# ScalarE copies a projection out of PSUM before VectorE convolves it

## The chip, the cores and the metric

The kernel runs on one core of a Trainium2 chip. The metric is the device time of one execution in microseconds (us); before, the median of three executions is 715.25 us. One execution was also taken by the hardware profiler, and every row shown here is from that one.

Five engines work side by side, each on a queue of its own, in order: TensorE (PE in the rows, its weight loads PEld), VectorE (DVE), ScalarE (ACT), GpSimd (POOL), and SyncE (SP), which issues the DMAs. An engine waits for another at a semaphore. PE writes its results into PSUM; ACT and DVE read them from there, POOL can't.

## The reference, cut to what matters

Two decoder layers over 256 tokens of width 1024. Each projects its input x, and part of that projection (q, k and v of a gated delta rule, four heads of 128 columns each) goes through a causal convolution of width 4 and a SiLU:

```
proj = x @ w_in
qkv  = silu(causal_dwconv(concat(q, k, v), conv_w))      # conv_w: 4 taps per column
beta, g = gates(a_logit, b_logit)
o_a  = gated_delta_rule(l2norm(q), l2norm(k), v, g, beta) # chunks, a triangular solve
o_b  = block-sparse softmax attention (partial rotary, own block)
x    = LN(alpha * x + concat(o_a, o_b) @ w_out)
x    = LN(alpha * x + (silu(gate) * val) @ w_down)        # gate, val: conv of width 3 of x @ w_up
```

## The kernel before, in words

Each layer has a mixing stage (projections, delta rule, attention, output projection) and a feed-forward stage. All 256 tokens are held at once: a projection (`proj`) makes one 128 x 256 result, the 128 columns of one head on the partitions and the tokens along the free dimension, in 24 matmuls. Operands are split into a high and a low part (`xh`, `xl`, `wh`, `wl`), so that three products of a fast format give the precision; ACT makes the high part of each weight chunk (line 196) and DVE or POOL the low part (line 197), two instructions of 512 columns each. Five chunks of `wh` and of `wl` can be ready ahead.

Results of projections lie in the PSUM pool `pj`, which has two buffers. So a projection can start only when the one two before it has been read out for the last time.

`gdn_conv` (lines 421 to 430) convolves one result, and it runs 24 times: 4 heads each of k, v and q in 2 layers. ACT writes `cv`, the result times the last tap (L424). DVE adds the other three taps one after the other, each reading the result in PSUM shifted by one to three tokens (L427, three instructions of 255, 254 and 253 columns). ACT takes a tanh of `cv` (L429), and DVE writes `dst` (L430), a slice of `ka`, `va` or `qa`; `va` is the tile that the rows name vz.

What follows on k: products of k with itself (`u_kk`), their scaled form (`u_am`), which goes through DRAM into the triangular solve of 16 x 16 blocks (`u_solve`): 28 small instructions a layer on POOL (L527, L529) and a copy (L530). Its result goes to DRAM (`dx`, L531) and back (L538), is spread by DVE (`u_ex`, L543), and then PE can put the blocks together (`u_lt`, L560, and what follows). POOL also does the second half of the rotary step (L455, L456) and half of the gate's cumulative products (L418).

The order of work is written out: `ORDER` lists the units of each layer, and `@` with letters says on which engines a unit must come behind the one before it. Where no letter binds, the order of the instructions on an engine is decided when the program is built, by what is expected to be ready first; the rows show DVE working weight splits (L197) in between the convolution steps.

Of the kernel before, what the change touches and what calls it, by code (L numbers as in the profile page):

```python
# [16 lines left out]
AF = mybir.ActivationFunctionType  # L17
OP = mybir.AluOpType
# [5 lines left out]
S = 256  # L24
# [65 lines left out]
def hybrid_kernel(ctx, tc, xT, x, wab, wch, par, lnrow, cst, msk, out):  # L90
    nc = tc.nc
    pe, act, dve, pool, sp = nc.tensor, nc.scalar, nc.vector, nc.gpsimd, nc.sync
# [20 lines left out]
    def ps_p():  # L113
        return ps_w()[:, 0:S]
# [226 lines left out]
    for l in range(DEPTH):  # L341
# [10 lines left out]
        def mt(name, shape, bufs=1, dt=F32):  # L352
            return (early if name in EARLY else mix).tile(shape, dt, name=name, bufs=bufs)
# [67 lines left out]
        def gdn_conv(ps, ct, dst):  # L421
            w = pr[:, P_GCONV + 4 * ct:P_GCONV + 4 * ct + 4]
            cv = mt("cv", [128, S], 2)
            act.activation(cv, ps, AF.Copy, scale=w[:, 3:4])  # L424
            for j in (2, 1, 0):
                o = 3 - j
                dve.scalar_tensor_tensor(cv[:, o:], ps[:, :S - o], w[:, j:j + 1], cv[:, o:], op0=OP.mult, op1=OP.add)  # L427
            th = mt("th", [128, S], 2)
            act.activation(th, cv, AF.Tanh, scale=0.5)  # L429
            dve.scalar_tensor_tensor(dst, th, 1.0, cv, op0=OP.add, op1=OP.mult)  # L430

        def u_conv(c0, ct, dst, h):
            ps = ps_p()
            proj(ps, l, c0 + h)
            gdn_conv(ps, ct + h, dst[:, h, :])
# [449 lines left out]
        for j in range(2, FJ):  # L885
            cs = []
            for gi in range(2):
                ps = ps_p() if j > 2 or gi else head
# [115 lines left out]
```

## Time and profile before

| | |
|---|---|
| median of three executions | 715.25 us (714.67 to 718.54) |
| the profiled execution | 714.04 us |
| its span, first to last instruction | 712.3 us |
| PE, DVE, ACT, POOL busy | 97%, 81%, 56%, 28% of the span |
| mean granted TensorE clock | 0.984 of full speed |

The profiled execution took 1.7 us more than its span, and 1.2 us less than the median. A share of busy time is a mean over stages with different limits, and a busy PE is not always PE at its full speed: matmuls overlap, and at half clock they last longer.

### The profile page before, as it was taken

What the parts mean: (1) busy time and instruction counts of PE and PEld (TensorE: products, weight loads), DVE (VectorE), ACT (ScalarE), POOL (GpSimd) and SP (SyncE); (2) the same over time, 40 slices, a digit from 0 to 9 for tenths busy, and PEclk for the clock granted to TensorE, in tenths of its full rate; (3) what the DMA queues carried; (4) which work ended last, traced back from release to release, by engine and by line L of the source; (5) the groups of instructions that cost most, each with busy time, mean ns of one, the idle gap of its engine ahead of it and who ended that gap; (6) DMA issues with size and microseconds to landing.
All of it is one profiled execution on the core that took longest, in us unless ns stands there. A gap on an engine that the chain in (4) does not pass through costs nothing.

```text
span 712.3 us, 13664 instructions
## 1 busy us (share of the span) xinstructions
PE 688.6 (97%) x5056; PEld 618.6 (87%) x5056; DVE 576.9 (81%) x1273; ACT 400.8 (56%) x908; POOL 197.2 (28%) x200
## 2 busy tenths in 40 slices
PE   8989999999999999999999989999999999999994
PEld 5979888787999999999888988888789999999994
DVE  5899877599788887778879987776998888887756
ACT  5644466546666665656355445556476566666531
POOL 0045700013333343332002382000153333333413
PEclk9999999999999999999999997999999999999998
DMA  8876351521766665656153437134246766666201
GB/s 313 305 244 192 78 198 40 199 89 61 276 220 194 211 222 184 202 181 205 60 201 129 144 94 222 61 103 159 66 150 234 233 213 194 214 206 202 70 1 60
DMA packets 41217, 118.07 MB, mean 166 GB/s; under 512 B 10176, under 2 KB 12992, under 8 KB 40640
## 3 DMA queue, kind: packets, MB, share of 16 engines
q1 hardware_dynamic: 41152, 117.21, 49.6%
q8 instruction: 40, 0.66, 0.3%
q14 instruction: 25, 0.20, 0.1%
HBM read 114.84 MB, written 2.36 MB: 165 GB/s over the span
## 4 chain that ended last, share of the span: by engine, by line
PE 86%; DVE 9%; ACT 1%; issue 1%; DMA 1%; SPq 0%; DVEq 0%; ACTq 0%
PE pj L211 16%; PE pj L212 15%; PE pj L214 15%; PE ac L732 8%; PE ac L733 8%; PE ac L734 8%; DVE wl L197 3%; PE pj L225 1%; PE pj L222 1%; DVE cv L427 1%; PE mx L619 1%; PE pj L223 1%; PE mx L313 1%; DMA wr<-in_wch_dram 1%; PE mx L662 1%
## 5 line engine op out<-in xcount | busy, mean ns | idle before, releaser
L196 ACT ACTIVATE wh<-wr 128x512 fp32r<-128x512 f32 x376 | 219.5, 622 | 108.2 <-PE pj L212 49.1
L211 PE MATMUL pj<-xh,wh 128*128 128x256 f32 x1024 | 258.6, 289 | 7.4 <-DVE cv L427 7.4
L212 PE MATMUL pj<-xl,wh 128*128 128x256 f32 x1024 | 257.2, 287 | 0.0
L197 DVE TENSOR_TENSOR wl<-wr,wh 128x512 fp32r<-128x512 f32 x292 | 206.7, 736 | 28.2 <-ACT wh L196 14.7
L211 PEld LDWEIGHTS pj<-xh,wh 128*128 128x128 f32 x1024 | 198.6, 194 | 11.4 <-issue 5.4
L212 PEld LDWEIGHTS pj<-xl,wh 128*128 128x128 f32 x1024 | 199.1, 194 | 1.6
L197 POOL TENSOR_TENSOR wl<-wr,wh 128x512 fp32r<-128x512 f32 x84 | 116.2, 1405 | 204.9 <-ACT wh L196 199.7
L214 PE MATMUL pj<-xh,wl 128*128 128x256 f32 x1024 | 147.6, 286 | 0.0
L214 PEld LDWEIGHTS pj<-xh,wl 128*128 128x128 f32 x1024 | 134.2, 194 | 0.4 <-issue 0.2
L733 PE MATMUL ac<-wh,fal 128*128 128x512 f32 x144 | 56.4, 392 | 0.0
L732 PE MATMUL ac<-wh,fah 128*128 128x512 f32 x144 | 56.1, 392 | 0.0
L734 PE MATMUL ac<-wl,fah 128*128 128x512 f32 x144 | 56.0, 389 | 0.0
L842 DVE TENSOR_TENSOR fal<-fth,fah 128x256 fp32r<-128x256 f32 (+1 forms) x48 | 36.8, 767 | 17.3 <-ACT fah L841 17.0
L828 DVE SCALAR_TENSOR_TENSOR fc<-pj,par,fc 128x255 f32<-128x255 f32 x80 | 38.1, 476 | 4.2 <-ACT fc L824 2.8
L828 DVE SCALAR_TENSOR_TENSOR fc<-pj,hw,fc 128x255 f32<-128x255 f32 x80 | 38.3, 478 | 3.7 <-ACT fc L824 2.4
L817 POOL TENSOR_SCALAR hw<-par 128x66 f32<-128x66 f32 x2 | 2.1, 1048 | 139.2 <-DVE wlh L197 139.2
L839 DVE SCALAR_TENSOR_TENSOR fth<-fth,fc 128x256 f32<-128x256 f32 (+1 forms) x48 | 23.6, 492 | 20.1 <-ACT fth L838 20.1
L841 ACT ACTIVATE fah<-fth 128x256 fp32r<-128x256 f32 (+1 forms) x48 | 18.9, 393 | 34.8 <-DVE fth L840 34.8
L838 ACT ACTIVATE fth<-fc 128x256 f32<-128x256 f32 (+1 forms) x48 | 19.2, 400 | 31.7 <-DVE fc L828 31.5
L427 DVE SCALAR_TENSOR_TENSOR cv<-pj,par,cv 128x255 f32<-128x255 f32 (+2 forms) x72 | 33.8, 472 | 0.6 <-ACT cv L424 0.3
L734 PEld LDWEIGHTS ac<-wl,fah 128*128 128x128 f32 x144 | 27.1, 188 | 5.9
L732 PEld LDWEIGHTS ac<-wh,fah 128*128 128x128 f32 x144 | 27.1, 189 | 4.8
(257 smaller groups left out, 1030.5 us busy)
## 6 DMA issues: line engine op xcount, KB each, us to landing
wr<-in_wch_dram SPq DMA_DIRECT2D x195, 512.0 KB, 4.1
lnb<-in_lnrow_dram SPq DMA_DIRECT2D x4, 1024.0 KB, 4.6
xres<-in_x_dram SPq DMA_DIRECT2D x2, 512.0 KB, 6.8
da<-A SPq DMA_DIRECT2D x4, 256.0 KB, 3.4
ka<-in_wch_dram SPq DMA_DIRECT2D x2, 512.0 KB, 4.5
qa<-in_wch_dram SPq DMA_DIRECT2D x2, 512.0 KB, 5.1
qb<-in_wch_dram SPq DMA_DIRECT2D x2, 512.0 KB, 4.8
kb<-in_wch_dram SPq DMA_DIRECT2D x2, 512.0 KB, 5.7
```

The costliest lines, as they stand in the source:

```text
L196: ih = act.activation(h[:, s], raw[:, s], AF.Copy)
L197: il = le.tensor_tensor(lo[:, s], raw[:, s], h[:, s].bitcast(F32), op=OP.subtract)
L211: pe.matmul(ps, h[:, k, :], xh[:, k, :], start=k == 0, stop=False)
L212: pe.matmul(ps, h[:, k, :], xl[:, k, :], start=False, stop=False)
L214: pe.matmul(ps, lo[:, k, :], xh[:, k, :], start=False, stop=k == KT - 1)
L427: dve.scalar_tensor_tensor(cv[:, o:], ps[:, :S - o], w[:, j:j + 1], cv[:, o:], op0=OP.mult, op1=OP.add)
L732: pe.matmul(ps, a_h, w_h[:, ns], start=start and i == 0, stop=False, skip_group_check=True)
L733: pe.matmul(ps, a_l, w_h[:, ns], start=False, stop=False, skip_group_check=True)
L734: pe.matmul(ps, a_h, w_l[:, ns], start=False, stop=stop and i == len(items) - 1, skip_group_check=True)
L828: dve.scalar_tensor_tensor(cv[:, d], ps[:, d.start - o:d.stop - o], w[:, q:q + 1], cv[:, d], op0=OP.mult, op1=OP.add)
L839: dve.scalar_tensor_tensor(th, th, 1.0, cg[:, ts], op0=OP.add, op1=OP.mult)
L842: dve.tensor_tensor(al, th, ah.bitcast(F32), op=OP.subtract)
```

## The change

ACT first copies the whole result from PSUM into `dst`, then makes `cv` as before. The three DVE steps read the copy in `dst` (SBUF) in place of PSUM. The last step overwrites `dst` as before. Nothing else is changed, `ORDER` and the convolution of the feed-forward stage (`ffn_conv`, L828) included.

```
         def gdn_conv(ps, ct, dst):
             w = pr[:, P_GCONV + 4 * ct:P_GCONV + 4 * ct + 4]
             cv = mt("cv", [128, S], 2)
+            act.activation(dst, ps, AF.Copy)
             act.activation(cv, ps, AF.Copy, scale=w[:, 3:4])
             for j in (2, 1, 0):
                 o = 3 - j
-                dve.scalar_tensor_tensor(cv[:, o:], ps[:, :S - o], w[:, j:j + 1], cv[:, o:], op0=OP.mult, op1=OP.add)
+                dve.scalar_tensor_tensor(cv[:, o:], dst[:, :S - o], w[:, j:j + 1], cv[:, o:], op0=OP.mult, op1=OP.add)
             th = mt("th", [128, S], 2)
             act.activation(th, cv, AF.Tanh, scale=0.5)
             dve.scalar_tensor_tensor(dst, th, 1.0, cv, op0=OP.add, op1=OP.mult)
```

## Rows read from the trace of the kernel before

**Rows 1.** Windows: us, then busy us per engine, granted clock, DMA share, GB/s.

```profile
20.00:70.00 50.00, 48.13 (x373) 45.67 (x371) 49.25 (x139) 28.13 (x62) 18.87 (x17) 1.00 0.72 241
...
500.00:695.00 195.00, 194.71 (x1318) 179.74 (x1317) 158.97 (x294) 114.85 (x233) 62.36 (x47) 1.00 0.50 162
```

**Rows 2.** Costliest groups: busy us, mean ns, idle before and its releasers.

```profile
L211 PE MATMUL pj<-xh,wh 128*128 128x256 f32 x1024 | 258.6, 289 | 7.4 <-DVE cv L427 7.4
...
L427 DVE SCALAR_TENSOR_TENSOR cv<-pj,par,cv 128x255 f32<-128x255 f32 (+2 forms) x72 | 33.8, 472 | 0.6 <-ACT cv L424 0.3
```

**Rows 3.** Timeline of PE: start, us, instruction, idle before it and its releaser.

```profile
72.05 0.43 PE L211 MATMUL pj<-xh,wh 128*128 128x256 f32 x1 [2.08 <-DVE cv L427]
...
419.14 0.36 PE L211 MATMUL pj<-xh,wh 128*128 128x256 f32 x1 [2.04 <-DVE cv L427]
...
435.45 0.36 PE L211 MATMUL pj<-xh,wh 128*128 128x256 f32 x1 [1.48 <-DVE cv L427]
```

**Rows 4.** Windows behind those three waits, columns as in rows 1.

```profile
72.00:76.00 4.00, 3.95 (x20) 3.98 (x21) 2.79 (x6) 1.05 (x3) 3.29 (x10) 0.57 0.14 53
420.00:424.00 4.00, 4.00 (x23) 3.73 (x22) 2.15 (x5) 1.46 (x3) 3.22 (x11) 0.57 0.03 6
437.00:447.00 10.00, 10.00 (x151) 9.34 (x148) 6.55 (x21) 4.97 (x17) 0.00 (x0) 0.52 0.72 264
```

**Rows 5.** Timeline of ACT, ahead of the first of those waits.

```profile
67.28 0.46 ACT L424 ACTIVATE cv<-pj,par 128x256 f32<-128x256 f32 x1
```

**Rows 6.** Single lines of the kernel: ns min/median/max, first and last start, forms.

```profile
L427 DVE SCALAR_TENSOR_TENSOR cv<-pj,par,cv x72: 463/471/484, 24.3 to 459.4; 128x255 f32<-128x255 f32 x24, 128x254 f32<-128x254 f32 x24, 128x253 f32<-128x253 f32 x24
...
L721 DVE SCALAR_TENSOR_TENSOR PT<-mx,par,zs x4: 737/740/741, 146.9 to 497.9; 128x512 f32<-128x512 f32 x4
...
L271 DVE SCALAR_TENSOR_TENSOR xres<-xres,lnr,lnb x14: 740/748/923, 159.5 to 708.4; 128x512 f32<-128x512 f32 x14
...
L442 DVE SCALAR_TENSOR_TENSOR zs<-th,pj x8: 407/412/420, 111.4 to 495.1; 128x256 f32<-128x256 f32 x8
...
L430 DVE SCALAR_TENSOR_TENSOR vz<-th,cv x8: 408/464/566, 72.4 to 433.5; 128x256 f32<-128x256 f32 x8
...
L450 DVE TENSOR_TENSOR kb<-kb,kt x8: 419/884/1005, 45.2 to 405.9; 128x256 f32<-128x256 f32 x8
...
L447 ACT ACTIVATE qb<-pj x8: 363/366/383, 30.2 to 411.5; 128x256 f32<-128x256 f32 x8
```

**Rows 7.** Windows of line 427 alone: DVE busy us (count), clock, DMA share, GB/s.

```profile
36.09:39.56 3.47, 1.33 (x3) 1.00 0.34 137
66.06:81.72 15.66, 4.68 (x10) 0.89 0.23 71
81.78:86.81 5.03, 2.36 (x5) 1.00 0.48 128
```

**Rows 8.** Timeline of POOL within the solve of the first layer.

```profile
74.13 0.29 POOL L529 TENSOR_TENSOR P<-P,T 64x50 f32<-64x50 f32 x1
...
78.11 0.36 POOL L529 TENSOR_TENSOR P<-P,T 64x50 f32<-64x50 f32 x1
...
78.87 0.61 POOL L529 TENSOR_TENSOR P<-P,T 64x44 f32<-64x44 f32 x1
```

**Rows 9.** Timeline of DVE beside four POOL instructions of the second layer.

```profile
430.20 3.00 DVE L197 TENSOR_TENSOR wl<-wr,wh 128x512 fp32r<-128x512 f32 x1
```

**Rows 10.** Timeline of SP: the solve's result is fetched.

```profile
85.32 0.38 SPq L538 DMA_DIRECT2D PT<-dx  x1
...
432.32 0.38 SPq L538 DMA_DIRECT2D PT<-dx  x1
```

**Rows 11.** That line's DMAs, from issue to landing.

```profile
DMA to landing us min/median/max: 3.2/3.3/3.3
```

**Rows 12.** Timeline of DVE: the result is spread, in each layer.

```profile
90.98 0.42 DVE L543 TENSOR_TENSOR gX<-PT,kt 128x256 f32<-128x256 f32 x1
...
436.19 0.42 DVE L543 TENSOR_TENSOR gX<-PT,kt 128x256 f32<-128x256 f32 x1
```

More of the change, by code (lines that the diff above doesn't have):

```diff
@@ L423, in gdn_conv @@
             cv = mt("cv", [128, S], 2)
+            act.activation(dst, ps, AF.Copy)
             act.activation(cv, ps, AF.Copy, scale=w[:, 3:4])
@@ L426, in gdn_conv @@
                 o = 3 - j
-                dve.scalar_tensor_tensor(cv[:, o:], ps[:, :S - o], w[:, j:j + 1], cv[:, o:], op0=OP.mult, op1=OP.add)
+                dve.scalar_tensor_tensor(cv[:, o:], dst[:, :S - o], w[:, j:j + 1], cv[:, o:], op0=OP.mult, op1=OP.add)
             th = mt("th", [128, S], 2)
```

## The prediction

> **What bounds the kernel now.** I read the windows by stage first. In the feed-forward stage PE is busy for 194.71 of 195 us at full clock, and nothing of the change runs there [rows 1]. All 24 convolutions lie in the mixing stages. In the first 50 us of the first one DVE is busy for 49.25 us and PE for 48.13 [rows 1]: two engines at their limit, DVE a little more so. The reader should keep that in mind, because a PE that is let go earlier there gains only what DVE can follow.
>
> The groups show the wait that the change is about. The first matmul of a projection stood idle for 7.4 us in all, and every bit of it was ended by L427, the convolution's last read of the PSUM buffer [rows 2]. The timeline of PE has the three large ones, 2.08, 2.04 and 1.48 us [rows 3]; smaller ones make up the other 1.8. Behind each of the three the granted clock is not 1.00 but 0.57, 0.57 and 0.52 [rows 4]: PE had been idle, and then runs mostly at 1.2 GHz instead of 2.4.
>
> **What the change removes: the wait for the buffer.** After it the last reader of the PSUM buffer is ACT's `cv`. Ahead of the first large wait, `cv` was made at 67.28 in 0.46 us [rows 5]; with a copy of 0.366 in front [rows 6] the buffer is free at 67.28 + 0.37 + 0.46 = 68.1, and PE, idle from 72.05 - 2.08 = 69.97 [rows 3], finds it free. So I expect all of these waits on DVE to go: 7.4 us. If PE isn't idle it should keep its clock: 4 x 0.43 = 1.7 us behind the first wait, 1.7 behind the second, 10 x 0.48 = 4.8 behind the third [rows 4]. The most that can be won is 7.4 + 3.4 + 4.8 = 15.6 us.
>
> **What holds PE next.** A little later in each layer PE needs the result of the solve, and that runs on POOL and through DRAM, not through the buffers. Its fetch was issued at 85.32 and 432.32 [rows 10], and landed 3.3 and 3.2 us later [rows 11], at 88.6 and 435.5. DVE spread it at 90.98 and 436.19 [rows 12]. So this gate can come forward by 2.4 us in the first layer and 0.7 in the second, 3.1 together, and no more. What else PE wins ahead of the gate is worth something only if later projections fill it. I take the 3.1 and half of the rest of waits and first two clock losses, (7.4 + 3.4 - 3.1) / 2 = 3.9, so 7.0. Of the 4.8 behind the third wait I take nothing: the gate of 436.19 lies just ahead of that stretch, and PE has to wait for it anyway.
>
> **What it adds on ACT.** 24 copies of 0.366 us, the price of L447, the same copy of the same shape [rows 6]: 8.8 us. ACT works for 28.13 of the 50 us [rows 1], so most are covered by its idle time. A copy delays the first DVE step only where DVE stands waiting for `cv`: 0.3 us of idle time in all 72 steps [rows 2], one place. I count one copy, 0.4 us; with all cover gone it would be 8.8. Behind the copy on ACT's queue stand `cv`, the weight splits and the tanh; the copy itself stands behind the tanh of the convolution before it, which waits for DVE, so a late DVE can still hold a buffer through ACT.
>
> **What it does to a DVE step.** A step takes 471 ns, and it reads PSUM, SBUF and a per-partition tap [rows 6]. The same operation on 512 columns with such a per-partition scalar takes 740 ns with one input in PSUM (L721) and at least 740, 748 in the middle, with both in SBUF (L271). Without that scalar it takes 407 at least with an input in PSUM (L442) and 408 with none (L430) [rows 6]. So the 63 ns between 471 and 408 go with the scalar, not with PSUM, and I price the move at 0; if they did go with PSUM, 72 x 0.063 = 4.5 us of DVE would fall away. The Trainium skill says the opposite: VectorE: DVE Perf Modes, "The TRN2 errata", lists 58 cycles of fixed cost from SBUF against 120 from PSUM, by which a step would lose 65 ns, an estimate, and the sum below 4.7 us. The pairs of rows don't bear it out.
>
> **What a step is now exposed to.** Reading PSUM, no step of 72 took longer than 484 ns [rows 6], though many ran beside POOL. DVE instructions with both inputs in SBUF do take longer there: L450, started just where POOL does its rotary step, has 419 at best and 884 in the middle [rows 6], and one weight split beside four POOL instructions in a row took 3.00 us [rows 9]. Here the Trainium skill agrees: SBUF — State Buffer, "Who interferes with whom", has a VectorE instruction with two SBUF inputs shut out while GpSimd reads SBUF, and the other way round. It speaks against this change, and these rows have it too.
>
> Counting the steps beside POOL: in the first layer 3 beside L418, 10 beside the solve, 5 beside its copy and the rotary step [rows 7]. In the second layer the same windows hold 3, 10 and 2. That is 13 beside large POOL instructions and 20 beside small ones. A large one costs 884 - 419 = 465 ns if DVE loses, 0 if POOL yields: 0 to 6.0 us. I take half, 3.0. A small one costs 464 - 408 = 56 ns (L430 on vz, which lies in the solve [rows 6]), up to 1.1 us; I take 0.6, because DVE has slack in part of that stretch.
>
> POOL loses as well. In the solve a POOL instruction takes 0.29 us alone, 0.36 beside L430 and 0.61 beside a weight split [rows 8]. Twenty more instructions like L430 make the solve later by 20 x 0.07 = 1.4 us over both layers; if each cost what a weight split costs, 20 x 0.32 = 6.4. A step has L430's columns, so I take 1.4, all of it on the gate.
>
> **The sum.** 714.04 - 7.0 + 0.4 + 0.0 + 3.0 + 0.6 + 1.4 = 712.4 us for an execution like the profiled one; the median lies 1.2 above it, so 713.6. A measurement of this kernel can tell about 0.5%, 3.6 us, from no change; this is 0.2%, no change. The order on each engine is decided anew at the build from what should be ready, so single instructions will trade places; I have no row for that and let the range carry it.
>
> **The rivals.** *The solve becomes late (slower).* If POOL gets to the port only between DVE's instructions, the solve takes 3.2 us longer in each layer, past the slack of 2.4 and 0.7: 0.8 + 2.5 = 3.3 us. The 6 steps beside L418 and the rotary step behind it lie ahead of the products that feed the solve, 6 x 0.465 = 2.8. PE, earlier or not, waits at the gate: 714.04 + 3.3 + 2.8 + 0.4 = 720.5, median 721.7. For it: L450's 884 and the 3.00. Against: L430 beside the solve lost only 56 ns. It decides once the solve is later by more than the slack, 3.1 us over both layers.
>
> *The buffers were the bound (faster).* PE's 7.4 and 3.4 us are won in full, because projections fill PE up to the gate and DVE spreads the result as soon as it lands: 714.04 - 10.8 + 0.4 + 3.0 + 0.6 = 707.2, median 708.4. For it: PE's waits had no other releaser. Against: DVE's 49.25 of 50 us.
>
> *The steps get shorter (faster).* PSUM, not the scalar, is what costs 63 ns: 4.5 us less on the engine that is at its limit, median 709.1. Against it stand the two pairs in rows 6. It is what the Trainium skill's table of fixed costs in VectorE: DVE Perf Modes would do here.
>
> **How the numbers follow.** Forecast 0.44, late solve 0.26, buffers 0.20, shorter steps 0.10. The forecast's own range is 708.5 to 718.5: bounds of the port's price, 3.0 either way, and the order, some 2 more. Of its 0.44, 0.07 lies below the 0.5% and 0.05 above. Faster: 0.07 + 0.19 + 0.08 = 0.34; slower: 0.05 + 0.23 = 0.28; the rest, 0.38, within. The range takes in the middles of the rivals: 705.5, 2.9 below the buffers' time, since the 4.8 of the third clock loss may come in part, to 722.0.
>
> **What would show it.** Right: no wait of PE on L427's successor, and clock 1.00 behind where the first two waits were; the copy at about 0.366 us x24; steps of 471 ns at best, with some of 0.7 to 1 us beside POOL; L543 between 89 and 92 and near 436. Wrong: steps near 410 ns (shorter steps); a solve that ends over 1.6 us later in a layer and a PE idle ahead of L560 (late solve); L543 well ahead of those times, or PE's saving kept to the end of the mixing stage (buffers); or another order on DVE that delays the products of k.

## The result, and the profile after

| | before | after |
|---|---|---|
| median | 715.12 us (4 executions) | 725.91 us (725.06 to 727.29, 4 executions) |
| ratio after / before | | 1.0148, 95% interval 1.0123 to 1.0173 |
| profiled execution, its span | 714.04, 712.3 us | 726.01, 724.2 us |
| mean granted clock | 0.984 | 0.975 |

The change makes the kernel 10.8 us slower, 3.9 us above the range's upper end. Throughout, ratios leave out executions over 1.5% slower than the fastest of their kernel (only three of g2's ten are), and medians are of all of them. In the changed kernel the lines behind 423 have numbers higher by one: the copy is L424, `cv` L425, a step L428, `dst` L431, the solve L528, L530 and its copy L531, the fetch L539, the spreading L544, and the gate of PE L561.

The waits on the buffers are gone. The group that answers to [rows 2], from the page of the changed kernel:

```profile
L211 PE MATMUL pj<-xh,wh 128*128 128x256 f32 x1024 | 259.0, 289 | 1.8 <-ACT cv L425 1.8
```

None of the 7.4 us that DVE ended is left; ACT ends 1.8. But PE waits longer than before, in another place. Its waits, summed by line, with the number of times and the longest:

```profile
PE ac L561 <- DVE gX L544: 14.9, 2, 8.7
```

and in PE's timeline, idle time and releaser in brackets:

```profile
92.52 0.96 PE L561 MATMUL ac<-gX,A 64*64 64x32 f32 x14 [6.18 <-DVE gX L544]
...
447.07 0.43 PE L561 MATMUL ac<-gX,A 64*64 64x32 f32 x4 [8.75 <-DVE gX L544]
```

Before, PE came to this gate with 0.03 and 0.15 us of idle time. Windows of all engines behind it, columns as in [rows 1]; the granted clock follows the five busy times:

```profile
92.00:96.00 4.00, 3.48 (x38) 3.13 (x38) 3.96 (x11) 1.23 (x4) 0.00 (x0) 0.50 1.00 389
96.00:104.00 8.00, 8.00 (x121) 7.67 (x122) 3.57 (x12) 4.13 (x17) 0.00 (x0) 0.50 0.46 174
104.00:110.00 6.00, 6.00 (x102) 4.61 (x102) 3.32 (x9) 4.14 (x12) 0.00 (x0) 0.98 0.00 0
447.00:456.00 9.00, 8.93 (x146) 8.25 (x147) 6.92 (x22) 4.23 (x16) 0.00 (x0) 0.50 0.88 322
456.00:460.00 4.00, 4.00 (x24) 3.87 (x24) 1.38 (x3) 1.27 (x3) 0.00 (x0) 0.59 0.00 0
```

In layer 1 the clock was 1.00 from 92 to 110 us before; now PE is at 1.2 GHz for 12 us. In layer 2 it ran at half clock before as well [rows 4], now for some 2 us more (12.2 us from the gate on, against 10.2).

The gate is late because the solve is. POOL's timeline: first instructions and closing copy of the solve in both layers, after:

```profile
66.18 1.20 POOL L528 TENSOR_TENSOR T<-T,P 64x14 f32<-64x14 f32 x1 [2.71 <-DVE P L525]
67.46 3.56 POOL L530 TENSOR_TENSOR P<-P,T 64x14 f32<-64x14 f32 x1
...
84.89 0.97 POOL L531 COPY P<-P 64x256 f32<-64x256 f32 x1
...
420.77 0.60 POOL L528 TENSOR_TENSOR T<-T,P 64x14 f32<-64x14 f32 x1 [0.92 <-DVE P L525]
...
439.60 0.84 POOL L531 COPY P<-P 64x256 f32<-64x256 f32 x1
```

and the same of the kernel before, not shown yet:

```profile
66.06 2.14 POOL L527 TENSOR_TENSOR T<-T,P 64x14 f32<-64x14 f32 x1 [1.88 <-DVE P L524]
...
81.78 1.07 POOL L530 COPY P<-P 64x256 f32<-64x256 f32 x1
...
412.82 0.60 POOL L527 TENSOR_TENSOR T<-T,P 64x14 f32<-64x14 f32 x1 [1.07 <-DVE P L524]
...
428.80 1.07 POOL L530 COPY P<-P 64x256 f32<-64x256 f32 x1
```

From the first start to the copy's end: 85.86 - 66.18 = 19.68 and 440.44 - 420.77 = 19.67 us after, 16.79 and 17.05 before: 2.89 and 2.62 longer, 5.5 together. In layer 1 the gate had a slack of 2.4 us (DMA landed at 88.6, spreading at 90.98 [rows 11, 12]); now the spreading follows the DMA at once. DVE's own queue ahead of it ended at 91.89 us, 0.1 us before the DMA landed at 92.0, so in layer 1 both were late. The fetch and the spreading, from SP's and DVE's timelines, answering to [rows 10] and [rows 12]:

```profile
88.32 0.38 SPq L539 DMA_DIRECT2D PT<-dx  x1
...
442.89 0.38 SPq L539 DMA_DIRECT2D PT<-dx  x1
```

```profile
92.04 0.42 DVE L544 TENSOR_TENSOR gX<-PT,kt 128x256 f32<-128x256 f32 x1
...
440.52 2.93 DVE L431 SCALAR_TENSOR_TENSOR qa<-th,cv 128x256 f32<-128x256 f32 x1 [0.54 <-ACT th L430]
446.59 0.42 DVE L544 TENSOR_TENSOR gX<-PT,kt 128x256 f32<-128x256 f32 x1 [3.13 <-DMA PT<-dx]
```

The first operation of layer 1's first norm, on DVE, before and after:

```profile
154.26 0.68 DVE L246 SCALAR_TENSOR_TENSOR xres<-xres,ac 128x512 f32<-128x512 f32 x1
...
160.67 0.68 DVE L246 SCALAR_TENSOR_TENSOR xres<-xres,ac 128x512 f32<-128x512 f32 x1
```

So the 12.0 us between the spans (712.26 and 724.24 us) lie here: first gate 92.04 - 90.98 = 1.1; from it to that norm 5.3 (68.6 against 63.3 us), the way that holds the stretch at half clock; from there to the second gate 4.0, of which the solve is 2.6 and the products of k ahead of it 1.5; behind the second gate 1.6 (277.65 against 276.07). From layer 1's norm to the start of layer 2 it is 212.8 us in both.

The steps themselves, as single lines (ns min/median/max), beside POOL's two lines of the solve after, and the same two before:

```profile
L428 DVE SCALAR_TENSOR_TENSOR cv<-ka,par,cv x24: 468/476/1256, 23.8 to 396.0; 128x255 f32<-128x255 f32 x8, 128x254 f32<-128x254 f32 x8, 128x253 f32<-128x253 f32 x8
L428 DVE SCALAR_TENSOR_TENSOR cv<-vz,par,cv x24: 469/483/522, 70.3 to 436.4; 128x255 f32<-128x255 f32 x8, 128x254 f32<-128x254 f32 x8, 128x253 f32<-128x253 f32 x8
L428 DVE SCALAR_TENSOR_TENSOR cv<-qa,par,cv x24: 471/480/485, 83.2 to 471.5; 128x255 f32<-128x255 f32 x8, 128x254 f32<-128x254 f32 x8, 128x253 f32<-128x253 f32 x8
...
L530 POOL TENSOR_TENSOR P<-P,T x28: 298/461/3562, 67.5 to 439.1; 64x14 f32<-64x14 f32 x4, 64x26 f32<-64x26 f32 x4, 64x36 f32<-64x36 f32 x4, 64x44 f32<-64x44 f32 x4
...
L528 POOL TENSOR_TENSOR T<-T,P x28: 289/418/2781, 66.2 to 438.7; 64x14 f32<-64x14 f32 x4, 64x26 f32<-64x26 f32 x4, 64x36 f32<-64x36 f32 x4, 64x44 f32<-64x44 f32 x4
```

```profile
L529 POOL TENSOR_TENSOR P<-P,T x28: 209/320/1829, 68.3 to 428.5; 64x14 f32<-64x14 f32 x4, 64x26 f32<-64x26 f32 x4, 64x36 f32<-64x36 f32 x4, 64x44 f32<-64x44 f32 x4
...
L527 POOL TENSOR_TENSOR T<-T,P x28: 225/274/2139, 66.1 to 428.2; 64x14 f32<-64x14 f32 x4, 64x26 f32<-64x26 f32 x4, 64x36 f32<-64x36 f32 x4, 64x44 f32<-64x44 f32 x4
```

In the median a step is no shorter than the 471 ns of [rows 6]; DVE pays 5 to 12 ns of a step, and POOL's medians rise from 320 to 461 and from 274 to 418 ns.

### The profile page after: what moved, and what is told of

Its sections match the earlier page's. It is cut to its first block, busy times and chain, and to the rows that moved or that the text cites. A ratio compares the mean times of both kernels' runs of the same rounds, so it can differ in the third digit from the quotient of the medians.

```text
span 724.2 us, 13666 instructions
## 1 busy us (share of the span) xinstructions
PE 689.3 (95%) x5056; PEld 621.0 (86%) x5056; DVE 585.3 (81%) x1273; ACT 407.4 (56%) x932; POOL 203.4 (28%) x200
## 4 chain that ended last, share of the span: by engine, by line
PE 82%; DVE 7%; POOL 5%; DMA 3%; issue 1%; ACT 1%; SPq 0%; DVEq 0%; ACTq 0%
PE pj L211 14%; PE pj L214 14%; PE pj L212 14%; PE ac L733 8%; PE ac L734 8%; PE ac L735 8%; POOL P L530 2%; POOL T L528 2%; DVE wl L197 2%; DVE cv L428 2%; PE pj L225 1%; PE pj L222 1%; PE pj L223 1%; PE mx L313 1%; PE mx L620 1%
## 5 line engine op out<-in xcount | busy, mean ns | idle before, releaser
L839 ACT ACTIVATE fth<-fc 128x256 f32<-128x256 f32 (+1 forms) x48 | 19.2, 400 | 32.6 <-DVE fc L829 32.5
L734 PEld LDWEIGHTS ac<-wh,fal 128*128 128x128 f32 x144 | 27.2, 189 | 4.5 <-DVE fal L843 0.2
```

The source lines that it names most:

```text
L734: pe.matmul(ps, a_l, w_h[:, ns], start=False, stop=False, skip_group_check=True)
L839: act.activation(th, cg[:, ts], AF.Tanh, scale=0.5)
```

## The experiments

Theory A: a step with both inputs in SBUF holds POOL up, the solve ends late, and PE, let go early, stands idle at the gate and loses its clock. Theory B: the order that the build chose is what costs. Theory C: the copies cost by themselves. "Solve" is the time from the end of DVE's mask ahead of the solve to the end of POOL's copy, "idle" PE's idle time ahead of its first matmul behind the gate, each for layer 1 and 2.

| kernel | solve us | idle us | median us | ratio to before, 95% |
|---|---|---|---|---|
| before | 16.9, 17.1 | 0.0, 0.1 | 714.2 to 716.3 | |
| after | 19.8, 19.8 | 6.2, 8.7 | 725.9 | 1.0148 (1.0123 to 1.0173) |
| e1_copy_only | 17.0, 16.4 | 0.0, 0.0 | 715.5 | 1.0032 (0.9998 to 1.0066) |
| e2_v_from_psum | 16.3, 18.1 | 0.0, 3.9 | 726.7 | 1.0170 (1.0143 to 1.0198) |
| e3_v_by_copy | 19.7, 19.3 | 4.7, 7.7 | 723.4 | 1.0125 (1.0105 to 1.0146) |
| f1_change_old_order | 19.7, 19.6 | 4.7, 7.8 | 725.1 | 1.0121 (1.0082 to 1.0160) |
| f2_before_new_order | 15.8, 16.8 | 0.5, 2.2 | 717.4 | 1.0020 (0.9992 to 1.0048) |
| f4_v_psum_old_order | 16.9, 18.1 | 1.4, 4.2 | 720.6 | 1.0069 (1.0042 to 1.0097) |
| e6_cv_in_psum | 17.5, 16.1 | 4.9, 5.5 | 729.1 | 1.0163 (1.0105 to 1.0222) |
| e4_after_fill | 19.8, 19.8 | 4.3, 4.0 | 733.5 | 1.0270 (1.0245 to 1.0295) |
| g1_after_fill | 19.8, 19.8 | 0.1, 0.2 | 719.9 | 1.0083 (1.0052 to 1.0115) |
| g2_cv_psum_fill | 17.5, 16.1 | 0.3, 0.0 | 717.3 | 1.0003 (0.9964 to 1.0041) |
| g3_before_fill | 17.9, 17.9 | 0.1, 1.7 | 715.6 | 1.0016 (0.9991 to 1.0041) |
| i1_after_z_ahead | 19.6, 19.2 | 2.3, 2.4 | 752.3 | 1.0497 (1.0457 to 1.0538) |
| i2_cv_psum_z_ahead | 17.9, 16.6 | 1.9, 3.5 | 742.9 | 1.0378 (1.0328 to 1.0427) |
| i3_cv_psum_one_z | 17.9, 17.1 | 2.8, 3.8 | 733.4 | 1.0257 (1.0196 to 1.0319) |
| j1_before_qa0_behind | 17.0, 16.4 | 0.1, 0.0 | 718.7 | 1.0030 (1.0002 to 1.0059) |
| j2_after_qa0_behind | 19.4, 19.8 | 9.1, 8.5 | 727.5 | 1.0162 (1.0132 to 1.0191) |

### Which part of the change costs

**e1_copy_only** keeps the copies, with the steps reading PSUM:

```
+            act.activation(dst, ps, AF.Copy)
             act.activation(cv, ps, AF.Copy, scale=w[:, 3:4])
...
                 dve.scalar_tensor_tensor(cv[:, o:], ps[:, :S - o], w[:, j:j + 1], cv[:, o:], op0=OP.mult, op1=OP.add)
```

> The ScalarE copies of PSUM into the result's tile stay, but VectorE's steps go on reading PSUM, so that the buffers come free as late as before the change. Theory A (steps with both inputs in SBUF slow GpSimd's solve, and the gate behind it opens late): the solve takes about 17 us in each layer again (19.75 after the change), PE meets the gate as before, and the time is 714 to 717 us. Theory B (the order in which the scheduler lays out the instructions is what changed the time): part of the loss stays, 718 us or more, with a solve of 17 us. Theory C (the copies themselves load ScalarE): most of the 10.8 us of loss stays, 722 us or more.

The solve is back to 17.0 and 16.4 us and the time within 0.7% of before: theory C falls, up to the 0.66% that the interval leaves. Two of its ten executions, 722.4 and 723.4 us at a mean clock of 0.97, lie near the change. Two things are seen besides. Its gates open later than before (PE's first matmul behind them at 92.82 and 441.23 us, against 91.45 and 436.66) at no cost, since PE had work up to them: a late gate alone is no loss where PE has work to do until then. And this kernel also keeps the buffers as late as before, so it doesn't tell the second SBUF input from the early buffers; e6 does.

**e2_v_from_psum** and **e3_v_by_copy** split the 24 convolutions. Those of v, four in each layer (the expectations say eight, which is both layers), lie beside the solve:

```
+            src = ps if 4 * 2 <= ct < 4 * 3 else dst      # e2; in e3 the two names change places
+            if src is dst:
+                act.activation(dst, ps, AF.Copy)
...
-                dve.scalar_tensor_tensor(cv[:, o:], ps[:, :S - o], w[:, j:j + 1], cv[:, o:], op0=OP.mult, op1=OP.add)
+                dve.scalar_tensor_tensor(cv[:, o:], src[:, :S - o], w[:, j:j + 1], cv[:, o:], op0=OP.mult, op1=OP.add)
```

> Only the convolutions of k and q go by the copy; the eight of v in a layer, whose steps lie beside the solve, read PSUM as before the change. Theory A: the solve is back at 17 to 17.5 us in each layer, and 5 us or more of the 10.8 us of loss go, so 714 to 720 us. Theory B or C: the solve can be back, but the time stays within 3 us of the changed kernel's 726.

> The complement: only v's eight convolutions of a layer go by the copy, k and q read PSUM. Theory A: the solve takes 19 to 20 us as after the change, and at least half of the loss is there, 720 to 726 us. Theory B or C: with a third of the copies, a third of the loss or less, 715 to 719 us, whatever the solve takes.

e3 is as A has it: v alone brings the long solve and 8.7 us (723.4 against 714.7 beside it). e2 is not: its solve is short in layer 1, yet it is as slow as the change. There DVE spread the solve's result at 96.57 us, though the DMA had landed at 88.2. DVE was still at q's steps and weight splits, in an order that the build had chosen for this kernel, and one closing step of v had taken 3.63 us beside POOL (82.02 us). So order had to be separated from the operands.

### The order of the instructions

In the next three kernels the order on PE, DVE, ACT and POOL is written out and enforced, instruction by instruction:

```
+def keep_order(nc, tc, nosync):
+    for name, text in QUEUES.items():          # one list of positions for each engine
...
+        for a, b in zip(order, order[1:]):
+            tc.add_manual_dep(ins[b], ins[a].name, nosync, reason="kept order")
```

**f1_change_old_order** is the change in the order of before, **f2_before_new_order** the kernel before in the order of after, and **f4_v_psum_old_order** is e2 in the order of before.

> The change, with the order of all instructions of PE, VectorE, ScalarE and GpSimd fixed to that of the kernel before (the 24 copies stand just ahead of the ScalarE instruction that they preceded). Theory A (the steps' second SBUF input slows GpSimd's solve and with it the gate): the solve takes about 19.7 us in each layer, and the time is 718 to 726 us. Theory B (the order that the build chose is what costs): the solve may be long, but the time is 713 to 717 us.

> The kernel before, without the copies, with the order of all instructions of PE, VectorE, ScalarE and GpSimd fixed to that of the changed kernel. Theory A: the solve takes about 17 us, and the time stays at 713 to 719 us (buffers come free later than the order assumes, some us of waits). Theory B: 722 us or more, with a solve of 17 us and PE idle or waiting ahead of the gate.

> Copies for k and q alone (v's convolutions read PSUM), with the order of the kernel before. In its own order this kernel took 726.7 us although its solve of layer 1 took only 16.3 us. Theory A with the order as a second cause: the solve takes 16 to 17.5 us in both layers and the time is 711 to 716 us. If the copies of k and q cost in another way than by the order, the time stays above 720 us.

f1 loses 1.2% with no instruction out of its old place, and f2 0.2%, which can't be told from nothing. Theory B falls for the change. PE at f1's two gates, and the windows behind them:

```profile
94.57 0.42 PE L673 MATMUL ac<-gX,A 64*64 64x32 f32 x3 [4.65 <-DVE gX L656]
...
447.94 0.42 PE L673 MATMUL ac<-gX,A 64*64 64x32 f32 x4 [7.80 <-DVE gX L656]
```

```profile
94.00:104.00 10.00, 9.43 (x148) 8.76 (x149) 6.05 (x17) 5.67 (x21) 0.00 (x0) 0.50 0.82 302
448.00:456.00 8.00, 8.00 (x142) 7.32 (x143) 5.11 (x14) 4.05 (x15) 0.00 (x0) 0.50 0.95 359
```

f4 stands between, against the 711 to 716 expected: 6 us faster than e2, so e2's order had cost that much, but still 0.7% slower than before. DVE's timeline at the end of the solve in both layers, and POOL's rotary step beside it:

```profile
84.01 3.00 DVE L309 TENSOR_TENSOR wl<-wr,wh 128x512 fp32r<-128x512 f32 x1
...
433.22 3.62 DVE L542 SCALAR_TENSOR_TENSOR cv<-qa,par,cv 128x254 f32<-128x254 f32 x1
```

```profile
85.03 1.43 POOL L571 TENSOR_TENSOR qb<-qb,sw 128x256 f32<-128x256 f32 x2
...
435.14 1.41 POOL L571 TENSOR_TENSOR qb<-qb,sw 128x256 f32<-128x256 f32 x2
```

Here it is DVE that is held. In layer 2 a step of q, 0.47 us elsewhere, took 3.62 and ended 0.3 us after POOL's run of large instructions; the spreading there came with its DMA (440.0 us) all the same. In layer 1 the one held was a weight split, as in layer 2 of the kernel before [rows 9], and the first spreading stands at 93.19 us, though the DMA had landed at 89.5. So the copies of q explain one long step, and what f4's 0.7% consists of stays open.

### The second SBUF input

**e6_cv_in_psum** is the change with the steps' sum in PSUM, so that each step has one input in SBUF:

```
-            cv = mt("cv", [128, S], 2)
+            cv = ps_a()[:, 0:S]
```

> The change, but the tile in which the steps add up lies in PSUM in place of SBUF, so that each step has one input in SBUF and one in PSUM; the order is the build's own. Theory A: no instruction of the solve is held up by a convolution step, the solve takes 16 to 17.5 us. If the solve alone carried the loss, the time is 713 to 718 us; if the order carries a part, the time stays at 719 us or more.

The solve is as short as before the change; its line and PE's gate:

```profile
L530 POOL TENSOR_TENSOR P<-P,T x28: 212/298/2428, 69.1 to 436.9; 64x14 f32<-64x14 f32 x4, 64x26 f32<-64x26 f32 x4, 64x36 f32<-64x36 f32 x4, 64x44 f32<-64x44 f32 x4
```

```profile
90.52 0.29 PE L561 MATMUL ac<-gX,A 64*64 64x32 f32 x2 [4.89 <-DVE gX L544]
...
444.29 0.32 PE L561 MATMUL ac<-gX,A 64*64 64x32 f32 x2 [5.52 <-DVE gX L544]
```

Against the change, two things differ: the place of the sum (the tanh and the closing step read it there too) and whatever the build made of the order. The long solve is gone. The Trainium skill (SBUF — State Buffer, "Who interferes with whom") has a VectorE instruction with two SBUF inputs contend with a GpSimd instruction that reads SBUF. The trace agrees: the median of POOL's L530 is 461 ns with steps of two SBUF inputs, 298 with steps of one. But the time did not fall. In layer 1 the spreading comes 0.9 us earlier than in the kernel before (90.05 us), PE is there 4.9 us too early, and the windows behind both gates are at half clock, with PE busy:

```profile
90.50:110.00 19.50, 19.27 (x274) 15.01 (x275) 9.40 (x26) 8.56 (x28) 0.00 (x0) 0.50 0.44 173
...
444.00:468.00 24.00, 23.19 (x292) 19.08 (x292) 12.19 (x33) 9.66 (x31) 0.00 (x0) 0.50 0.35 127
```

From the spreading to the next norm it takes 72.8 and 78.3 us in the two layers, against 63.3 and 69.6 before. So buffers that come free early lose as much without a long solve as with it: the long solve isn't needed for the loss.

### Idle time and the clock

Matmuls of zeros, put into PE's queue, add work and take none away:

```
+            bank = ps_a()
+            for _ in range(N_FILL[l]):
+                pe.matmul(bank, zero[:, 0:128], zero, start=True, stop=True)
+            ps = bank[:, 0:256].rearrange("p (b h q i) -> p b h q i", b=2, h=HG, q=2)
```

In **e4_after_fill** the build places them; in **g1_after_fill** and **g2_cv_psum_fill** (e6) the order is enforced and they stand right ahead of L561; in **g3_before_fill** they stand ahead of the three projections of [rows 3].

> The changed kernel with extra matmuls of zeros (26 in layer 1 and 38 in layer 2, 128x512) laid into PE's queue ahead of the gate, where PE stood idle for 6.2 and 8.7 us and then ran at a granted clock of 0.50 for some 10 us. They add work only. If the half clock behind the gate is what the late gate costs (part of theory A), the clock behind the gate is 0.9 or more and the time falls by 4 to 8 us to 718 to 722; if the lateness of the gate alone is the cost, the time stays at 725 to 728.

> The changed kernel in its own order, with matmuls of zeros (27 in layer 1, 39 in layer 2, 128x512, about 0.22 us each) fixed into PE's queue right ahead of the gate, where it stood idle for 6.2 and 8.7 us. They add work only. In the earlier run with such matmuls the scheduler had moved a projection behind the gate, and idle gaps of 4.3 and 4.0 us were left. If the half clock behind the idle gap is a loss of its own: the granted clock from the gate on is 0.9 or more, the way from the gate to the first layer norm of layer 1 takes about 63 us as before the change (68.2 after it), and the time is 715 to 721 us. If the late gate alone costs the 10.8 us: 724 us or more.

> The kernel with the steps' sum in PSUM (729.1 us, solve 17.5 and 16.1 us, gate 0.9 us earlier than before the change in layer 1), in its own order, with 22 and 25 matmuls of zeros right ahead of the gate, where PE stood idle for 4.9 and 5.5 us. If its whole loss is the half clock behind the gate (0.50 over 92 to 110 and 450 to 470 us), the clock there is 0.9 or more and the time falls by about 19 us (9.5 and 9.3 us behind the two gates) to 706 to 712 us, below both kernels. If not, it stays above 720 us.

> The kernel before, in its own order, with matmuls of zeros in the three waits of PE on a projection's buffer that ended at 72.05 us (9 matmuls), 419.14 us (9) and 435.45 us (6), behind which the clock was 0.57, 0.57 and 0.52. If a wait costs more by the half clock behind it than by its length: the clock stays at 0.9 or more in the three places, 1.7 + 1.7 + about 4.8 us are won, and the time is 705 to 710 us. If not, 713 to 717 us.

e4 tells nothing of the clock: gaps of 4.3 and 4.0 us were left, and the clock from 92 to 110 us was 0.65; why it is slower than the change itself stays open. g1 has next to none (0.1 and 0.2 us), its timeline and windows:

```profile
87.50 5.78 PE L670 MATMUL ac<-zero 128*128 128x512 bf16 x26
93.38 0.30 PE L676 MATMUL ac<-gX,A 64*64 64x32 f32 x4
```

```profile
92.00:96.00 4.00, 3.90 (x47) 2.67 (x45) 3.46 (x11) 2.59 (x6) 0.00 (x0) 1.00 0.99 346
96.00:104.00 8.00, 6.52 (x123) 6.25 (x123) 4.20 (x14) 4.08 (x16) 0.00 (x0) 0.79 0.59 222
...
447.00:456.00 9.00, 9.00 (x187) 8.27 (x187) 7.19 (x22) 6.58 (x24) 0.00 (x0) 1.00 0.77 295
```

With the solve as long as after the change, about half of the loss goes: 1.0083 in place of 1.0148, 4.6 us by the ratios, 6.0 by the medians. It goes in the second layer for the most part:

```profile
159.95 0.68 DVE L357 SCALAR_TENSOR_TENSOR xres<-xres,ac 128x512 f32<-128x512 f32 x1
```

From the spreading at 92.90 us to this norm it is 67.0 us, against 68.6 after the change and 63.3 before, not the 63 expected: only 1.6 of layer 1's 5.3 came back, with half clock for 3.4 us in place of 12 and PE idle for a new 1.5 us (ahead of 99.53 us). From the second spreading to the next norm it is 65.8 us, against 70.8 after the change and 69.6 before: 5.0 came back, 3.8 of them beyond the kernel before, which runs at half clock there itself. That what is left, 0.83% or 5.9 us, is near the solve's 5.5 is therefore no proof of it.

g2 gives its answer by the clock. Its ten executions took 709.5 to 726.6 us: 709.5, 710.1 and 710.8 at a mean clock of 0.996, 716.5 to 718.3 in four at 0.983 to 0.985, 724.9 to 726.6 in three at 0.969 to 0.973. The expected 706 to 712 came at the highest mean clock, where by that mean it held in both layers; in the profiled one (726.6 us) it fell 6 us behind the first gate and 9 us behind the second, each time after PE had stood idle for a moment behind the gate (0.8 and 1.9 us). As a kernel it isn't faster than before.

g3 has full clock behind the first two waits of the kernel before, and is no faster:

```profile
72.00:76.00 4.00, 4.00 (x34) 3.75 (x34) 3.56 (x9) 2.32 (x6) 3.37 (x9) 1.00 0.05 16
420.00:424.00 4.00, 4.00 (x32) 3.75 (x33) 3.55 (x8) 2.53 (x6) 3.45 (x8) 1.00 0.02 6
437.00:447.00 10.00, 8.93 (x146) 8.25 (x147) 5.98 (x16) 5.59 (x19) 0.00 (x0) 0.56 0.85 311
```

What PE saves ahead of the gate is not won: in layer 2 it then idles at the gate (1.7 us), and the stretch behind it stays at half clock. The solve even took 17.9 us in both layers, 1.0 and 0.8 more than before, and the spreading came no earlier (91.08 and 437.60 us). So [rows 4]'s first two losses had been covered by the wait for the solve.

### Where the work lies

Can useful work fill the gap? **i1_after_z_ahead** moves two projections of z per layer ahead of the gate, in the changed kernel; **i2_cv_psum_z_ahead** does it in e6, **i3_cv_psum_one_z** with one of them. **j1_before_qa0_behind** and **j2_after_qa0_behind** move one projection of q in layer 1 the other way:

```
-... solve@G va:1@D qa:1 qa:0@P ex@DPA lt@GP ...
+... solve@G va:1@D z:0 z:2 qa:1 qa:0@P ex@DPA lt@GP ...     # i1, i2; z:0 alone in i3; layer 2 alike
+... solve@G va:1@D qa:1 ex@DPA lt@GP ... qa:0 qa:3@G ...    # j1, j2
```

> The changed kernel with two projections of z per layer placed ahead of the gate in the written order (PE needs some 5.8 us for them, and z has no convolution steps on VectorE), the rest left to the build. If PE's idle time at the gate and the clock behind it are what can be won back, PE idles 0 to 3 us at the gate, the granted clock there stays at 0.9 or more, and the time is 714 to 720 us, as with the matmuls of zeros (719.9) or better, since this work is useful. The solve stays at 19 to 20 us, so that the kernel before isn't beaten by more than 1 us. If the clock loss only moves behind the gate, where this work is then missing, 722 us or more.

> The same two projections of z per layer ahead of the gate, in the kernel with the steps' sum in PSUM (solve 16 to 17.5 us, PE idle 4.9 and 5.5 us at the gate, 729 us). If early buffers are a gain of their own once the solve is not held up and PE keeps its clock: 705 to 711 us, below the kernel before. If the idle time comes back behind the gate, where the two projections are missing: 716 us or more.

> One projection of z per layer ahead of the gate, in the same kernel: PE idles about 2 to 2.6 us at the gate. If the clock holds over an idle time of that length: 706 to 712 us. If it falls as behind the longer ones: 718 us or more.

> The kernel before, with the projection of q's first head in layer 1 moved from ahead of the gate to behind it in the written order. The runs with z ahead of the gate became slower by the work that was missing behind it; here the opposite is tried. VectorE's first operation at the gate stood at 90.98 us, 2.3 us after the DMA had landed, behind q's convolution steps and weight splits. If the gate is set there by VectorE's queue and the work is worth more behind the gate: the gate opens 1 to 2.5 us earlier and the time is 711 to 714 us. If PE then idles at the gate and loses its clock: 716 to 722 us.

> The same move in the changed kernel. There the gate is set by the solve and its DMA (landed at 92.01 us, VectorE's operation at 92.04 us), so it opens no earlier, and PE, which idled 6.2 us, idles some 9 us. If idle time ahead of the gate and work behind it weigh against each other, the time stays at 722 to 729 us.

Filling the gap with work from behind it was the worst of all. In i1 the spreading is 6.8 us behind its DMA, because DVE's queue ahead of it now waits for weights; its timeline and PE's waits:

```profile
92.01 1.29 DVE L197 TENSOR_TENSOR wl<-wr,wh 128x512 fp32r<-128x512 f32 x2 [5.75 <-ACT wh L196]
...
99.52 0.42 DVE L544 TENSOR_TENSOR gX<-PT,kt 128x256 f32<-128x256 f32 x1
```

```profile
PE mx L663 <- ACT P L634: 10.3, 4, 2.7
PE pj L211 <- DVE zs L443: 5.3, 3, 3.9
```

and behind the gate, where z is missing, PE waits for the attention (L663), at a granted clock of 0.54 and 0.52 over the 10 us behind the two gates. These causes weren't separated. Nor does the opposite help: j1 has its first gate 2.0 us earlier and is 0.3% slower, j2 stays where the change is. No kernel of these beats the one before.

## Why the prediction was wrong

- **The waits on the buffers go:** right, 7.4 us to nothing on DVE, 1.8 new on ACT. **The copies:** right, 0.368 to 0.384 us each, and for all of them 0.3% in e1, which can't be told from nothing.
- **A step keeps its duration:** right. The Trainium skill's table (VectorE: DVE Perf Modes, "The TRN2 errata") would have had it lose 65 ns, an estimate; the medians rose by 5 to 12, and the measurement decides.
- **What PE wins, 7.0 us:** this step failed. It let the gate come forward by 3.1 and had half of the rest filled by later projections. The gate came 1.1 us later in layer 1, and another 4.0 us later in layer 2, counted from layer 1's norm; what PE saved became idle time in front of it, 14.9 us. g3 gives PE the clock back and wins nothing; e6 lets PE go early without a long solve and wins nothing either. The waits on the buffers had been covered by the wait for the solve.
- **PE keeps its clock:** failed, and had no term on the other side. It does where the waits were (1.00 from 72 to 76 and from 420 to 424 us); at the gate it now loses it, for 12 us in layer 1 where none was lost before, and for 2 us more in layer 2.
- **POOL in the solve, 1.4 us:** measured 5.5. The prediction took 0.07 us a step, from one POOL instruction beside L430, and 20 steps; 15 steps lie in each solve, and 5.5 / 30 = 0.18. The upper price of 0.32 a step had bounded it. Not all of it is the steps': in layer 1 the first two instructions of the solve end 0.8 us later (71.02 - 66.18 against 70.10 - 66.06), beside weight splits and rotary products, ahead of the first step at 70.31. The count, from windows of L428 alone:

```profile
66.18:85.86 19.68, 7.22 (x15) 1.00 0.16 55
420.77:440.44 19.67, 7.30 (x15) 1.00 0.13 44
```

- **DVE beside large POOL instructions, 3.0:** the long ones are there (2.93 us above, a step of 1.26), but those at the solve's end lie under the DMA's flight: in layer 2 DVE waits 3.13 us for the DMA behind them, in layer 1, where two weight splits took 4.48 us, it is done 0.1 us before the DMA lands.
- **The rivals:** "the solve becomes late" named the place: 2.9 and 2.6 us longer against its 3.2, past its 3.1 in sum, and PE idle ahead of the gate. Its 721.7 lacked the clock. "The buffers were the bound" is not borne out by e6 and g3: buffers that come free early, without a late solve, bring the first gate 0.9 us forward, and full clock behind the buffer waits brings nothing. But the three executions of g2 at the highest clock (709.5 to 710.8 us, with the kernel before at 710.8 to 716.8 beside them) come near its 708.4, so with a short solve and a clock that holds it isn't excluded. "The steps get shorter" is refuted by the medians of 476 to 483 ns.

By place, of the 12.0 us between the spans: 1.1 by the later first gate, 5.3 behind it, 4.0 ahead of the second gate (solve and products of k), 1.6 behind that. Shown is that the order and the copies alone don't make the loss (f1, f2, e1), that the second SBUF input makes the solve long (e3, e6), and that a PE let go early loses its clock at the gate with a long solve or a short one (f1, e6). How the loss divides between the late solve and the clock is argued, not shown: of the median times, the long solve has 725.9 us without and 719.9 with matmuls of zeros in the gap, the short one 729.1 and 717.3. Left open is also how much of g1's gain is the clock and how much the order of PE's small matmuls behind the gate, and why i1 to i3 lose as much as they do.

## What to carry to other kernels

A wait that is removed ahead of a gate is won only if the gate moves: ask first what sets the gate, and whether the change slows that. Look at the granted clock behind an idle time too, and at what PE runs there: here 1.48 us of idle ahead of the small products at the gate was followed by 10 us at half clock, and 2.08 us ahead of projections by 3.4 us [rows 3, 4]. When a change also changes the order that a build chooses, fix the order in both kernels before blaming either.

## What the hardware showed unexpectedly

- Half clock outlasts the idle time by far, with PE busy: after 4.89 us of idle, 19.27 of 19.5 us busy at 0.50 (e6). The length of the idle time alone doesn't tell how long: after 2.08 us the clock was 0.57 over 4 us, after 1.48 us 0.52 over 10 us [rows 3, 4], and after 1.71 us in e1 (PE's wait that ended at 421.63 us) it was 1.00. Matmuls of zeros in the gap kept it at 1.00 behind the gate of g1's layer 2; in layer 1 it was 1.00 for 4 us and 0.79 over the next 8.
- A 64x14 instruction of POOL took 3.56 us beside a run of DVE's weight splits and rotary products, and 0.45 at the end of the same solve; a 0.47 us step of DVE took 3.62 beside a run of POOL's (f4). Each of the two was held while the other ran back to back.
- In the medians DVE paid 5 to 12 ns a step for what cost POOL some 140 ns an instruction.
